# A selective-scan layer whose group loop is tied chunk by chunk: context products in mid tile, the second x tile turned into scan buffers, six stores in place of twenty

## The chip, the core and the metric

The kernel runs on one core of a Trainium2 chip. The core has five engines that run side by side, each through its own queue in order: TensorE (PE in the profile; PEld is its weight load), VectorE (DVE), ScalarE (ACT), GpSimd (POOL) and SyncE (SP), which here issues DMA transfers. The metric is the device time of one execution, in microseconds (us).

## The reference

One attention layer and one bidirectional state-space (SSD) layer over 1024 latent positions, with 256 context positions ahead of them, model width 1024. The change lies in the SSD layer, which is, cut to what matters:

```python
z, xbc, dt_raw = jnp.split(h @ w_in, ...)              # front, for context and latent
xbc = silu(centred_depthwise_conv(xbc, conv_w, conv_b))   # 5 taps
xs, bm, cm = jnp.split(xbc, ...)                       # 8 groups: x 256, B 128, C 128 columns each
dt = softplus(dt_raw + dt_bias)
# per direction d, in chunks of 128 positions:
a_cs   = jnp.cumsum(dt * A, axis=chunk);  a_last = a_cs[:, :, -1]
states = einsum(bm, exp(a_last - a_cs), xs * dt)
h      = exp(a_last) * h + states                      # from the context's final state
y      = einsum(cm @ bm.T * exp(a_cs_q - a_cs_s), xs * dt) + einsum(cm, h_prev, exp(a_cs))
u = rms_norm_per_group((y_fwd + y_bwd + d_skip * xs) * silu(z))
h = h + gate * ((u * norm_w) @ w_out)
```

## The kernel before

Everything is fp32; each product is made of three passes over a high and a low part (`uH`, `uL` of the input, `wh`, `wl` of the weights). Layer 0 and the making of `uH` and `uL` fill the span up to some 747 us and are not touched. Then comes the SSD layer in 8 groups of 4 heads.

A group has a *front* (function `front`) and a *scan* (`slot`, once for each of 8 chunks). The front makes four tiles, in the order `bT` (B), kind 0 and kind 1 (the two halves of x) and `cT` (C): for each but `cT` 24 products of 128x256 for the context into the one PSUM buffer `psD` (line 1085), and 48 products of 128x512 for the latent part into one of the two large buffers `pj2` (L1095, shown as pj). ScalarE and VectorE then apply the taps (L1007, L1011) and the SiLU (`silu`: a tanh on ScalarE back into the PSUM tile, L1018, and a product on VectorE, L1019), after which the PSUM tile's content is no longer wanted. The scan needs B and x with positions on partitions. So the tile is transposed on TensorE (L1058) and copied out by ScalarE (L1061): `natural` writes the transposes back into the tile's own `pj2` buffer, half a tile, copy, other half, copy. After the four tiles z follows, two times 96 products of 128x256 (L1129), each into a `pj2` buffer. So the first z tile needs the buffer of kind 1, and the second that of `cT`.

The scan of a chunk (`slot`) has on TensorE the scores product `pcb` (L1247), two products with the carried states `po` (L1249, L1250), the state product `S` (L1256), four products `yd` (L1281), and two transposes of the chunk before (L1312), all in the three small PSUM buffers `psX`; around them VectorE multiplies the decay tile `M` by the scores (L1251), merges two loaded rows into `M` (`merge`, L1230), GpSimd scales x (`xweight`, L1173) and states (`decay`, L1178), ScalarE takes exponentials of `M` (L1236). Context and backward states of a group (`states`: L1198 into `psD`, then the decay on GpSimd and an addition on VectorE, L1210) are made ahead, one at each `tick`.

The order: the front of group g+1 runs beside the scan of group g. `front` yields the cost of each product, and `run` takes products until a chunk's share is spent; a queue (`post`) pays out the work of the other engines as that cost grows, and work marked with a number (`LATE`, 3.0 us) comes out that much queue time later. This gives each instruction a place and priority; a scheduler then orders each engine's queue by priority and by when it reckons operands to be there, so rows move against the written order. `issue_after(x)` forbids the scheduler to put an instruction ahead of x. It is a rule on the order of issue; it adds no wait of its own.

The beginning of the layer is different: group 0's front runs alone, and beside it the step sizes dt are worked out (`dt_chain`). Their running sums go to DRAM in 8 stores (`decay`, L941), then come 12 small stores of the chunks' total decays (`total`, L951 and L952) and one load that spreads these over all partitions into `eal` (L953). Then `rows` loads M and bw of the first two chunks (L1221). The bw tiles get an offset on GpSimd (L1226) before they are merged.

Of the kernel before, what the change touches and what calls it, by code (L numbers as in the profile page):

```python
# [17 lines left out]
P = 128  # L18
# [15 lines left out]
R = 4  # L34
# [26 lines left out]
POST = 0.5  # L61
LATE = 3.0
DTPACE = 1.0
SEGS = (1.5, 2.0, 2.0, 2.2, 2.2)
# [47 lines left out]
class Kernel:  # L112
# [812 lines left out]
    def dt_chain(self, keep, rows):  # L925
# [11 lines left out]
        def decay():  # L937
            for o in (0, 384):
                for y in range(4):
                    d, s = y // 2, (o // 384) * 512 + 256 * (y % 2)  # L940
                    nc.sync.dma_start(self.acs_d[32 * d : 32 * d + 32, s : s + 256], w3[32 * y : 32 * y + 32, o : o + 256])  # L941
# [16 lines left out]
        def turn(b):  # L958
# [35 lines left out]
            lambda: act(ea, w3, AF.Exp),  # L994
            rows,
        ]
# [18 lines left out]
    def silu(self, raw, acc):  # L1015

        nc = self.nc
        return [lambda: nc.scalar.activation(raw, acc, AF.Tanh),  # L1018
                lambda: nc.vector.scalar_tensor_tensor(acc, in0=raw, scalar=1.0, in1=acc, op0=ALU.add, op1=ALU.mult)]  # L1019

    def front(self, g, st, post, first=None, dt=None):
# [30 lines left out]

        def natural(raw, acc, dst, o, n):
            steps = []

            def tr(lo, hi):
                for x in range(lo, hi):
                    nc.tensor.transpose(raw[:, x * P : (x + 1) * P], acc[:, x * P : (x + 1) * P], self.ident)  # L1058

            def ev(d, lo, hi):  # L1060
                nc.scalar.copy(d[:, :, o : o + P], raw[:, lo * P : hi * P].rearrange("p (c n) -> p c n", n=P))  # L1061

            for d, lo, hi in dst:
                steps.append(lambda lo=lo, hi=hi: tr(lo, hi))
                steps.append(lambda d=d, lo=lo, hi=hi: ev(d, lo, hi))
            return [(LATE, steps)]

# [8 lines left out]
        for n, (x, kind) in enumerate(tiles):  # L1076
# [3 lines left out]
            wh, wl = cur["h"], cur["l"]  # L1080
            if nat:
                raw = t(ps, [P, 512], F32, "psD")[:, :CTX]
                for k in range(KT):
                    for y, (l, r) in enumerate(((wh, uH), (wh, uL), (wl, uH))):
                        nc.tensor.matmul(raw, l[:, k, :], r[2][:, k, :], start=k + y == 0, stop=k == KT - 1 and y == 2)  # L1085
                        yield N256
                acc = t(pf, [P, CTX], F32, "cctx")
                post.extend(self.taps(x, raw, acc, 0, CTX, CTX) + self.silu(raw, acc) + natural(raw, acc, [(st[nat[0]][2], 0, 2)], nat[1], 2))
            raw = t(ps, [P, LAT], F32, "pj2")
            acc = t(pf, [P, LAT], F32, "cacc") if nat and kind != "bT" else t(p, [P, LAT], F32, kind)  # L1090
            for q in ((0,), (1,)) if g == 0 and n == 0 else ((0, 1),):
                for k in range(KT):
                    for y, (l, r) in enumerate(((wh, uH), (wh, uL), (wl, uH))):
                        for i in q:
                            nc.tensor.matmul(raw[:, 512 * i : 512 * i + 512], l[:, k, :], r[i][:, k, :], start=k + y == 0, stop=k == KT - 1 and y == 2)  # L1095
# [12 lines left out]
            post.extend(self.taps(x, raw, acc, 0, LAT, LAT) + self.silu(raw, acc))  # L1108
            if nat:
                post.extend(natural(raw, acc, [(st[nat[0]][i], 4 * i, 4 * i + 4) for i in range(2)], nat[1], 8))  # L1110

            def done(kind=kind, acc=acc):
                st[kind] = acc

            post.append((LATE, [done]) if nat else done)
        need(w)
        w0, w = w, loads[-1]()
        post.extend(w["steps"])
        for i in range(2):
            pj = t(ps, [P, 4, 256], F32, "pj2")  # L1120
            for q in range(2):
                ww = (w0, w)[q]
                need(ww)
                for c in range(4):
                    for k in range(4):
                        u, v = uH[i][:, 4 * q + k, c * P : (c + 1) * P], uL[i][:, 4 * q + k, c * P : (c + 1) * P]
                        for y, (l, r) in enumerate(((u, ww["h"]), (u, ww["l"]), (v, ww["h"]))):

                            nc.tensor.matmul(pj[:, c], l, r[:, k, :], start=c % 2 + q + k + y == 0, stop=c % 2 == 1 and q == 1 and k == 3 and y == 2)  # L1129
                            yield N256  # L1130
# [14 lines left out]
    def ssd(self, c0):  # L1145
# [31 lines left out]
        def decay(hn, h, g, c, d):  # L1177
            nc.gpsimd.tensor_tensor(hn, h, self.eal[:, hd(d, g), c].unsqueeze(2).broadcast_to([P, R, HP]), op=ALU.mult)  # L1178

# [58 lines left out]
        def slot(n, st, fill, tick):  # L1238
# [102 lines left out]
        offset(0, bw[0])  # L1341
        merge(fw[0], bw.pop(0))
        for half in range(2):
            decays(0, fw[0], half)
        self.tail = None
        with ExitStack():
            for g in range(G):
# [10 lines left out]
                def run(until):  # L1358
                    nonlocal spent
                    while spent < until:  # L1360
                        cost = next(work, None)
                        if cost is None:
                            return
                        spent += cost
                        post.run(cost)

# [22 lines left out]
    def ssd_out(self, p, spare, sp, sc, post):  # L1389
# [107 lines left out]
        for n, (i, mg, qs) in enumerate(sweeps):  # L1497
# [8 lines left out]
            for q in qs:  # L1506
# [5 lines left out]
                for z in range(2):  # L1512
# [11 lines left out]
                    for x in range(4):  # L1524
                        sl = slice(x * P, (x + 1) * P)
                        for y, (l, r) in enumerate(((w["h"], hi), (w["h"], lo), (w["l"], hi))):
                            nc.tensor.matmul(banks[x], l[:, z, sl], r, start=k == 2 * qs[0] and y == 0, stop=k == 2 * qs[-1] + 1 and y == 2)  # L1527
                            yield N512
# [165 lines left out]
```

## Time and profile before

| | us |
|---|---|
| median of three runs (1806.79, 1809.46, 1813.08) | 1809.46 |
| profiled execution | 1807.02 |
| its span | 1805.3 |
| around the span | 1.7 |

The span is what the profiler saw, from the first instruction to the last. Of the span, TensorE is busy 96%, VectorE 65%, ScalarE 48%, GpSimd 44%. A row such as "PE pj L1129 <- ACT xn L1061: 9.1, 7, 1.3" says that products of line 1129 waited for ScalarE's copy of line 1061, 9.1 us in all, 7 times, the longest 1.3 us. In a row of the chain stand the start, the length and the work: "1030.35 2.66 PE pj L1129 x20" are 20 products from 1030.35 us on. A row of stretches has, after its bounds, its length, then the busy time of PE, PEld, DVE, ACT and POOL, then the granted clock of TensorE (1.00 is full), the DMA share and rate.

### The profile page before, as it was taken

The page shows a single profiled execution, that of the slowest core. Times are in us where ns is not written, and L with a number is a line of the kernel's source. Part 1 is how long each engine was busy: PE and PEld are TensorE (multiplying, and loading weights), DVE is VectorE, ACT ScalarE, POOL GpSimd, SP SyncE. Part 2 cuts the span into 40 slices and gives each one's busy share as a digit, 9 for nine tenths or more (in the row PEclk, how much of TensorE's full clock was granted, in tenths as well). Part 3 has the DMA queues.
Part 4 walks back from the last instruction along what each step waited for, and adds up shares of the span by engine and source line. Part 5 has one row for each costly group of instructions (what it writes and reads, how often), then busy time and mean ns, then how long its engine had stood idle before and what let it go on. Part 6 is the DMA issues. An engine that isn't in the chain of part 4 may idle for free.

```text
span 1805.3 us, 28983 instructions
## 1 busy us (share of the span) xinstructions
PE 1739.6 (96%) x10319; PEld 1494.7 (83%) x10319; DVE 1181.8 (65%) x2115; ACT 867.1 (48%) x1906; POOL 799.0 (44%) x1068
## 2 busy tenths in 40 slices
PE   6899999999999999999999999999999999999997
PEld 2697788888888887778888898988889898888887
DVE  4634436778877885684776858577684867766734
ACT  3612237777777774452443525344353534544522
POOL 2331127555575545103454544645454464554411
PEclk9999999999999999999999999999999999999999
DMA  9558856444455436222222323222332322656533
GB/s 334 226 144 268 283 177 149 106 100 111 111 153 130 120 102 221 73 53 73 71 77 82 92 62 98 79 71 79 81 93 62 100 73 76 174 169 170 175 101 121
DMA packets 212495, 227.61 MB, mean 126 GB/s; under 512 B 16384, under 2 KB 149632, under 8 KB 212352
## 3 DMA queue, kind: packets, MB, share of 16 engines
q1 hardware_dynamic: 178288, 207.12, 38.0%
q0 software_dynamic: 34064, 18.65, 5.8%
q8 instruction: 81, 1.33, 0.3%
q14 instruction: 62, 0.51, 0.1%
HBM read 190.88 MB, written 35.13 MB: 125 GB/s over the span
## 4 chain that ended last, share of the span: by engine, by line
PE 81%; DVE 9%; ACT 4%; DMA 3%; issue 2%; SPq 1%; POOL 1%; DVEq 0%; ACTq 0%; POOLq 0%
PE pj L1095 17%; PE pj L1129 10%; PE pj L1527 7%; PE pj L246 6%; PE pj L247 6%; PE pj L248 6%; PE psD L1085 4%; PE psX L1281 3%; PE pt L684 3%; PE psD L1198 2%; PE pv L691 2%; PE pv L690 1%; PE S L659 1%; PE S L658 1%; PE psX L1249 1%
## 5 line engine op out<-in xcount | busy, mean ns | idle before, releaser
L246 PE MATMUL pj<-uH,wh 128*128 128x512 f32 (+1 forms) x712 | 257.4, 363 | 9.0 <-ACT uH L470 6.3
L247 PE MATMUL pj<-uL,wh 128*128 128x512 f32 (+1 forms) x712 | 243.3, 342 | 0.5 <-POOL uL L707 0.4
L248 PE MATMUL pj<-uH,wl 128*128 128x512 f32 (+1 forms) x712 | 242.4, 341 | 1.4 <-POOL wl L231 1.4
L1095 PE MATMUL pj<-uH,wl 128*128 128x512 f32 x512 | 172.7, 405 | 0.0
L1095 PE MATMUL pj<-uH,wh 128*128 128x512 f32 x512 | 171.4, 405 | 1.2 <-ACT bn L1061 0.7
L1095 PE MATMUL pj<-uL,wh 128*128 128x512 f32 x512 | 169.2, 402 | 0.0
L246 PEld LDWEIGHTS pj<-uH,wh 128*128 128x128 f32 x712 | 135.6, 191 | 36.2 <-ACT uH L470 7.7
L1129 PE MATMUL pj<-wh,uH 128*128 128x256 f32 x512 | 150.3, 294 | 9.1 <-ACT xn L1061 9.1
L1173 POOL TENSOR_TENSOR xw<-xn,dtdec 128x256 f32<-128x256 f32 x144 | 92.9, 650 | 141.6 <-PE psD L1198 107.1
L1129 PE MATMUL pj<-wh,uL 128*128 128x256 f32 x512 | 152.7, 298 | 0.0
L248 PEld LDWEIGHTS pj<-uH,wl 128*128 128x128 f32 x712 | 135.0, 190 | 18.6 <-POOL wl L231 2.3
L247 PEld LDWEIGHTS pj<-uL,wh 128*128 128x128 f32 x712 | 135.8, 191 | 16.0 <-issue 3.0
L1129 PE MATMUL pj<-wl,uH 128*128 128x256 f32 x512 | 146.7, 287 | 0.0
L689 DVE TENSOR_TENSOR pl<-pt,ph 128x512 fp32r<-128x512 f32 x168 | 114.1, 688 | 47.2 <-ACT ph L688 46.2
L231 POOL TENSOR_TENSOR wl<-wr,wh 128x512 fp32r<-128x512 f32 x76 | 100.2, 1322 | 86.1 <-ACT wh L229 85.2
L663 DVE CUSTOM_DVE_ANT_0 sm<-S,mask,nsink 128x640 f32<-128x640 f32 (+2 forms) x160 | 119.2, 773 | 19.8 <-PE S L659 12.6
L665 ACT ACTIVATE sm<-sm,nm 128x640 f32<-128x640 f32 (+2 forms) x160 | 118.6, 742 | 16.6 <-DVE nm L663 15.9
L688 ACT CAST ph<-pt 128x512 fp32r<-128x512 f32 x168 | 97.5, 586 | 56.0 <-PE pt L684 52.7
L229 ACT CAST wh<-wr 128x512 fp32r<-128x512 f32 (+1 forms) x116 | 74.7, 648 | 87.7 <-PE pj L247 63.5
L1095 PEld LDWEIGHTS pj<-uH,wl 128*128 128x128 f32 x512 | 95.3, 188 | 19.2
L1095 PEld LDWEIGHTS pj<-uL,wh 128*128 128x128 f32 x512 | 95.4, 188 | 18.7
L1129 PEld LDWEIGHTS pj<-wh,uH 128*128 128x128 f32 x512 | 98.7, 193 | 13.5 <-ACT xn L1061 12.1
(339 smaller groups left out, 4810.8 us busy)
## 6 DMA issues: line engine op xcount, KB each, us to landing
wr<-w_x SPq DMA_DIRECT2D x32, 512.0 KB, 4.6
M<-acs SPq DMA_DIRECT2D x64, 256.0 KB, 4.9
bw<-acs SPq DMA_DIRECT2D x64, 256.0 KB, 5.5
wr<-w_sk SPq DMA_DIRECT2D x24, 512.0 KB, 3.8
wr<-wg SPq DMA_DIRECT2D x40, 256.0 KB, 4.5
qs<-q POOLq DMA_DIRECT2D x40, 256.0 KB, 3.9
wada<-w_ada SPq DMA_DIRECT2D x16, 512.0 KB, 7.2
wr<-wq SPq DMA_DIRECT2D x32, 256.0 KB, 3.0
```

Source lines behind the costliest of these rows:

```text
L231: (eng or nc.vector).tensor_tensor(l, raw, h, op=ALU.subtract)
L246: self.nc.tensor.matmul(ps, lh, rh, start=first and i == 0, stop=False)
L247: self.nc.tensor.matmul(ps, lh, rl, start=False, stop=False)
L248: self.last_mm = self.nc.tensor.matmul(ps, ll, rh, start=False, stop=last and i == n - 1)
L663: nc.vector.tensor_tensor_reduce(out=sm[:, :W], in0=Sv, in1=self.mask[:, m0 : m0 + W], scale=-SCALE, scalar=self.nsink[:, 4 * j + r : 4 * ...
L665: nc.scalar.activation(sm[:, :W], sm[:, :W], AF.Exp, bias=nm[:, r : r + 1], scale=-1.0, accum_out=sums[:, r : r + 1])
L688: nc.scalar.copy(ph, ptf)
L689: nc.vector.tensor_sub(pl, ptf, ph)
L1095: nc.tensor.matmul(raw[:, 512 * i : 512 * i + 512], l[:, k, :], r[i][:, k, :], start=k + y == 0, stop=k == KT - 1 and y == 2)
L1129: nc.tensor.matmul(pj[:, c], l, r[:, k, :], start=c % 2 + q + k + y == 0, stop=c % 2 == 1 and q == 1 and k == 3 and y == 2)
L1173: nc.gpsimd.tensor_tensor(xw, X(st, c).rearrange("p (r h) -> p r h", r=R), self.dtdec[:, c, hd(d, g)].unsqueeze(2).broadcast_to([P, R, HP] ...
L1527: nc.tensor.matmul(banks[x], l[:, z, sl], r, start=k == 2 * qs[0] and y == 0, stop=k == 2 * qs[-1] + 1 and y == 2)
```

## The change

It has six parts.

1. `decay`: the running sums go out in 4 stores of 64 rows in place of 8 of 32; `total`: the totals in 2 stores in place of 12. `eal` then has its columns in another order, which `EPOS` gives.
2. `rows` (the first M and bw loads) stands right behind the stores of the sums, ahead of the totals and of the steps after them.
3. The first `merge` is tied behind the last SiLU product.
4. `natural`: all transposes of a tile, then its two copies. For kind 1 alone (`apart`) each half is transposed into a `psX` buffer of its own, so that its `pj2` buffer is free as soon as the SiLU product is done; that step, and the mark that the tile is there (`done`), come 6.8 us of queue time later (`LAST`) rather than 3.0.
5. The context products of a tile come in the middle of its latent products (after the fourth of eight steps) rather than ahead of them, but for the first tile.
6. The chunk's `pcb` is tied behind the last product of the front, and all front work of a chunk behind the chunk's `pcb`.

```diff
+LAST = 6.8
+EPOS = (0, 1, 5, 6, 3, 4, 8, 9, 2, 7)
...
         def decay():
-            for o in (0, 384):
-                for y in range(4):
-                    d, s = y // 2, (o // 384) * 512 + 256 * (y % 2)
-                    nc.sync.dma_start(self.acs_d[32 * d : 32 * d + 32, s : s + 256], w3[32 * y : 32 * y + 32, o : o + 256])
+            for d in range(2):
+                for o in range(2):
+                    dst = self.acs_d[32 * d : 32 * d + 32, 512 * o : 512 * o + 512].rearrange("r (h n) -> h r n", h=2)
+                    nc.sync.dma_start(dst, w3[64 * d : 64 * d + 64, 384 * o : 384 * o + 256])
...
             act(et, tot, AF.Exp)
-            for y in range(4):
-                d, h = y // 2, y % 2
-                row = self.eal_d[0][32 * d : 32 * d + 32]
-                for o, c in ((0, 2 * h), (3, 4 + 2 * h)):
-                    nc.sync.dma_start(row[:, c : c + 2], et[32 * y : 32 * y + 32, o : o + 2])
-                nc.sync.dma_start(row[:, 8 + h : 9 + h], et[32 * y : 32 * y + 32, 2:3])
+            for d in range(2):
+                nc.sync.dma_start(self.eal_d[0, 32 * d : 32 * d + 32].rearrange("r (h k) -> h r k", h=2), et[64 * d : 64 * d + 64])
...
             decay,
+            rows,
             total,
...
-            rows,
...
-        def natural(raw, acc, dst, o, n):
+        def natural(raw, acc, dst, o, n, apart=False):
...
+            def turn(d, lo, hi):
+                out, q = (t(ps, [P, 512], F32, "psX"), lo) if apart else (raw, 0)
                 for x in range(lo, hi):
-                    nc.tensor.transpose(raw[:, x * P : (x + 1) * P], acc[:, x * P : (x + 1) * P], self.ident)
...
+                    nc.tensor.transpose(out[:, (x - q) * P : (x - q + 1) * P], acc[:, x * P : (x + 1) * P], self.ident)
+                return lambda: nc.scalar.copy(d[:, :, o : o + P], out[:, (lo - q) * P : (hi - q) * P].rearrange("p (c n) -> p c n", n=P))
...
+            if apart:
+                for d, lo, hi in dst:
+                    out = []
+                    steps.append(lambda d=d, lo=lo, hi=hi, out=out: out.append(turn(d, lo, hi)))
+                    steps.append(lambda out=out: out[0]())
+            else:
+                out = []
+                steps.append(lambda: out.extend(turn(d, lo, hi) for d, lo, hi in dst))
+                steps += [lambda x=x: out[x]() for x in range(len(dst))]
+            return [(LAST if apart else LATE, steps)]
...
+            if nat and g + n == 0:
+                yield from ctx()
...
                 for k in range(KT):
+                    if k == KT // 2 and nat and g + n > 0:
+                        yield from ctx()
...
-            post.append((LATE, [done]) if nat else done)
+            post.append((LAST if kind == 1 else LATE, [done]) if nat else done)
...
-            nc.tensor.matmul(pcb, st["bT"][:, cs], st["cT"][:, cs], start=True, stop=True)
+            with self.tc.issue_after(self.pe.ins):
+                self.opened = nc.tensor.matmul(pcb, st["bT"][:, cs], st["cT"][:, cs], start=True, stop=True)
...
-        merge(fw[0], bw.pop(0))
+        with self.tc.issue_after(self.silu_last.ins):
+            merge(fw[0], bw.pop(0))
...
-                        cost = next(work, None)
...
+                        with self.tc.issue_after(self.opened.ins):
+                            cost = next(work, None)
```

`self.pe` is the latest product of a front (or of the closing product), `self.silu_last` the latest SiLU product. No arithmetic is added or taken away.

What this does to the queues. Below, a name's number tells buffers apart; line numbers after the change are some 1 to 12 higher. First, TensorE at the hand-over from `cT` to z while group 1's scan runs. Before (L1095 is `cT`, pj_2526 kind 1's buffer, psD_11038 its context, L1256 S, L1281 yd, L1247 pcb):

```order
L1256 MATMUL psX_11313<-xw_11263,bn_2266_9618 128x256
...
L1058 MATMUL pj_2526_11107<-ident_63,cacc_11108 128x128 x4
...
L1281 MATMUL psX_11342<-xn_2263_9615,M_11131 128x64 x2
L1058 MATMUL psD_11038<-ident_63,cctx_11106 128x128 x2
...
L1247 MATMUL psX_11464<-cT_10161,bT_9663 128x128
L1058 MATMUL pj_2526_11107<-ident_63,cacc_11108 128x128 x4
L1249 MATMUL psX_11466<-hf_11314,cT_10161 128x256
...
L1129 MATMUL pj_2582_11401<-wh_11295,uH_2034_8170 128x256
```

And after:

```order
L1209 MATMUL psD_11344<-xw_11310,bn_2461_10684 128x256
...
L1209 MATMUL psD_11373<-xw_11342,bn_2461_10684 128x256
L1060 MATMUL psX_11298<-ident_63,cacc_11029 128x128 x4
L1060 MATMUL psX_11304<-ident_63,cacc_11029 128x128 x4
L1293 MATMUL psX_11321<-xn_2265_9603,M_11101 128x64 x4
L1140 MATMUL pj_2582_11380<-wh_11273,uH_2034_8170 128x256
```

Before, the transposes of kind 1 stood in two pieces a dozen rows apart, both in the buffer that z (L1129) takes over; now both stand at the end of `cT`, in two psX buffers, directly ahead of `yd` and z.

Second, SyncE's queue behind the scans of the step sizes. Before:

```order
L941 DMA acs_8737<-sz_8871 32x256 x8
L951 DMA eald_8741<-tot_8874 32x2 x2
L952 DMA eald_8741<-tot_8874 32x1
...
L1221 DMA M_9099<-acs_8737 128x4x128
L1221 DMA bw_9101<-acs_8737 128x4x128
L953 DMA eal_8736<-eald_8741 128x640
```

After:

```order
L943 DMA acs_8737<-sz_8871 2x32x256 x4
L1232 DMA M_9005<-acs_8737 128x4x128
L1232 DMA bw_9007<-acs_8737 128x4x128
L1232 DMA M_9009<-acs_8737 128x4x128
L1232 DMA bw_9011<-acs_8737 128x4x128
L950 DMA eald_8741<-tot_8874 2x32x5 x2
L951 DMA eal_8736<-eald_8741 128x640
```

The first loads of M and bw moved from behind 20 stores to behind 4.

Third, TensorE in the first chunk of group 0's scan. Before, the last states (L1198) are spread over the z products and the next group's first tile:

```order
L1198 MATMUL psD_9443<-xw_9420,bn_2161_8760 128x256
...
L1247 MATMUL psX_9601<-cT_9227,bT_8798 128x128
...
L1198 MATMUL psD_9464<-xw_9441,bn_2161_8760 128x256
...
L1198 MATMUL psD_9489<-xw_9462,bn_2161_8760 128x256
L1256 MATMUL psX_9607<-xw_9487,bn_2161_8760 128x256
L1281 MATMUL psX_9644<-xn_2158_8757,M_9099 128x64 x4
```

After:

```order
L1209 MATMUL psD_9442<-xw_9419,bn_2162_8761 128x256
L1106 MATMUL pj_2271_9610<-uL_2133_8671,wh_9527 128x512
L1106 MATMUL pj_2271_9610<-uH_2034_8170,wl_9529 128x512
L1209 MATMUL psD_9467<-xw_9440,bn_2161_8760 128x256
L1209 MATMUL psD_9488<-xw_9465,bn_2161_8760 128x256
L1209 MATMUL psD_9509<-xw_9486,bn_2161_8760 128x256
L1268 MATMUL psX_9595<-xw_9507,bn_2161_8760 128x256
L1293 MATMUL psX_9628<-xn_2158_8757,M_9005 128x64 x4
L1262 MATMUL psX_9591<-hb_2253_9511,cT_9213 128x256
L1091 MATMUL psD_9665<-uH_1654_6747,wh_9527 128x256
```

Before, some 20 products stood between each two of the last three states; now the last three, all through the one psD buffer, stand row on row, and the next context products (L1091) want the same buffer right behind.

More of the change, by code (lines that the diff above doesn't have):

```diff
@@ L1109, in front @@
             if nat:
-                post.extend(natural(raw, acc, [(st[nat[0]][i], 4 * i, 4 * i + 4) for i in range(2)], nat[1], 8))
+                post.extend(natural(raw, acc, [(st[nat[0]][i], 4 * i, 4 * i + 4) for i in range(2)], nat[1], 8, kind == 1))
             def done(kind=kind, acc=acc):
                 st[kind] = acc
-            post.append((LATE, [done]) if nat else done)
+            post.append((LAST if kind == 1 else LATE, [done]) if nat else done)
         need(w)
@@ L1360, in run @@
                     while spent < until:
-                        cost = next(work, None)
[L1362 to L1365, printed above, removed]
+                        with self.tc.issue_after(self.opened.ins):
+                            cost = next(work, None)
+                            if cost is None:
+                                return
+                            spent += cost
+                            post.run(cost)
                 def tick():
@@ L1526, in ssd_out @@
                         for y, (l, r) in enumerate(((w["h"], hi), (w["h"], lo), (w["l"], hi))):
-                            nc.tensor.matmul(banks[x], l[:, z, sl], r, start=k == 2 * qs[0] and y == 0, stop=k == 2 * qs[-1] + 1 and y == 2)
+                            self.pe = nc.tensor.matmul(banks[x], l[:, z, sl], r, start=k == 2 * qs[0] and y == 0, stop=k == 2 * qs[-1] + 1 and y == 2)
                             yield N512
```

26 lines of the change are left out of this document (10 added, 16 removed).

## The prediction

> **What bounds the kernel now.** I read the page first, then the stretches of the SSD layer, then TensorE's waits in it, then the chain and the timelines at the two places where TensorE stands.
>
> ```profile
> span 1805.3 us, 28983 instructions
> PE 1739.6 (96%) x10319; PEld 1494.7 (83%) x10319; DVE 1181.8 (65%) x2115; ACT 867.1 (48%) x1906; POOL 799.0 (44%) x1068
> PE 81%; DVE 9%; ACT 4%; DMA 3%; issue 2%; SPq 1%; POOL 1%; DVEq 0%; ACTq 0%; POOLq 0%
> L1095 PE MATMUL pj<-uH,wh 128*128 128x512 f32 x512 | 171.4, 405 | 1.2 <-ACT bn L1061 0.7
> L1129 PE MATMUL pj<-wh,uH 128*128 128x256 f32 x512 | 150.3, 294 | 9.1 <-ACT xn L1061 9.1
> ```
>
> TensorE carries the chain, and no product is added or removed. So only time in which TensorE stands, or runs at a lower clock, can be won or lost. Where that is, the stretches of the SSD layer tell (the change acts from about 747 to 1735 us):
>
> ```profile
> 780.00:800.00 20.00, 17.12 (x91) 13.87 (x90) 19.07 (x25) 10.58 (x14) 0.00 (x0) 1.00 0.15 39
> 800.00:820.00 20.00, 16.25 (x83) 12.53 (x81) 12.30 (x19) 11.73 (x41) 2.78 (x4) 0.95 0.47 84
> 820.00:840.00 20.00, 20.00 (x140) 19.24 (x141) 8.64 (x10) 3.21 (x5) 6.86 (x12) 0.88 0.16 53
> ...
> 955.60:1061.40 105.80, 104.50 (x651) 93.63 (x651) 72.77 (x124) 45.10 (x106) 53.04 (x74) 1.00 0.29 80
> ...
> 1590.30:1735.00 144.70, 144.67 (x688) 119.96 (x688) 88.28 (x133) 64.16 (x128) 55.07 (x64) 1.00 0.52 159
> ```
>
> A group of the steady loop is 105.8 us, of which TensorE is busy 104.50: it stands 1.3 us. The last group and the closing product (1590 to 1735) have no gap to win. The beginning (780 to 820) has 2.9 and 3.75 us of standing, and a granted clock of 0.95 and 0.88 just behind it. TensorE's waits in that layer say the same:
>
> ```profile
> PE pj L1129 <- ACT xn L1061: 9.1, 7, 1.3
> PE pj L1058 <- DVE cacc L1019: 2.9, 2, 2.3
> ```
>
> Seven groups times 1.3 us is the one steady wait, z's first product behind a copy of the second x tile.
>
> **Part A: that tile turned into buffers of its own, and later.** The chain through one of the seven shows what z waits for:
>
> ```profile
> 1024.02 0.44 PE pj L1058 x4
> ...
> 1026.16 0.88 ACT M L1236 x3
> 1027.04 0.34 ACT uT L1313
> 1027.38 0.94 ACT wh L1034
> 1028.32 1.11 ACT cT L1007
> ...
> 1029.83 0.48 ACT xn L1061
> ...
> 1030.35 2.66 PE pj L1129 x20
> ```
>
> The second half's copy stands on ScalarE behind a weight cast, `cT`'s first tap and the rest, and z needs the buffer that it empties. After the change z needs only the SiLU product of that tile. When is that there? In the trace the tile's last product is issued at 1006.88 us, and then:
>
> ```profile
> 1006.88 0.24 PE pj L1095
> ...
> 1012.79 4.78 PE pj L1095 x21
> 1008.70 3.91 DVE L1011 SCALAR_TENSOR_TENSOR cacc<-pj,cw,cacc 128x1022 f32<-128x1022 f32 x3
> 1015.33 1.27 DVE L1011 SCALAR_TENSOR_TENSOR cacc<-pj,cw,cacc 128x1022 f32<-128x1022 f32 x1
> 1017.77 1.22 DVE L1019 SCALAR_TENSOR_TENSOR cacc<-pj,cacc 128x1024 f32<-128x1024 f32 x1
> ```
>
> The SiLU ends at 1018.99, 11.9 us behind the product's end at 1007.12. Its order on VectorE is little different after the change; I take 12.1. What TensorE has to do in that time: by the new order 48 products of `cT` at 4.78/21 = 0.228 us, 10.9, and of one chunk's scan `po`, `S` and two states (five products at 0.43, below), and the scores and three transposes, some 0.6 by four transposes' 0.44; together 13.7. So the transposes come about 1.6 us after their operand is there, and z behind them waits for nothing. The whole 9.1 us goes. The bounds: 0, if VectorE is over 2.9 us later than I count, and 10.3, because the pipeline also has to fill again behind each wait (the issue of products resumes 1.47 us late, not 1.3, as I read it from the starts on either side). I take 9.1, as the slack exceeds the difference of the two orders on VectorE. The two copies now hang behind the transposes, and what is late next is the next user of psX, a transposed y or the next `pcb`: by the order's rows they stand 4.8 and 5.6 us behind, cover enough for two copies of 0.48 us.
>
> **Part B: six stores, and the loads ahead of them.** In the beginning the chain leaves TensorE altogether:
>
> ```profile
> 795.98 0.42 SPq L941
> ...
> 803.40 3.08 DMA eald<-tot
> ...
> 807.07 9.10 DMA M<-acs
> ...
> 821.95 5.08 PE pj L1129 x30
> 827.46 3.83 PE pj L1129 x32
> POOL bw L1226 <- DMA bw<-acs: 72.6, 1, 72.6
> 815.05 0.73 DVE L1230 COPY_PREDICATED M<-before,bw 128x512 f32<-128x512 int32 x1 [5.26 <-POOL bw L1226]
> 815.92 1.22 DVE L1019 SCALAR_TENSOR_TENSOR cacc<-pj,cacc 128x1024 f32<-128x1024 f32 x1
> 814.26 0.62 PE L1095 MATMUL pj<-uH,wl 128*128 128x512 f32 x2
> 817.19 0.66 PE L1058 MATMUL pj<-ident,cacc 128*128 128x128 f32 x4 [2.31 <-DVE cacc L1019]
> ```
>
> The stores take SyncE from 795.9 to 803.4 us at 0.46 each (0.42 and the step to the next), the loads then need 9.1 us, GpSimd's offset and VectorE's merge wait for them, and behind the merge, in order, stands the SiLU of the second x tile. VectorE idles 5.26 us with that SiLU ready to run. TensorE has its last `cT` products out at about 814.7; then until 821.95 it does 8 transposes (0.44 for four), two of the context and two states (0.43 each), about 2.0 us of work in 7.2. So it loses 5.2 us there. After the change the merge stands behind the last SiLU, so this SiLU follows its taps, and the loads start 16 stores, some 7 us, earlier besides. z then waits for nothing. The gain: 5.2 us. The clock behind it: 30 products in 5.08 us at 0.169 each, against 32 in 3.83 at 0.120 right after: 30 x 0.049 = 1.5 us. If the stall goes, so does the dip; I take 1.1 of the 1.5, since the first products behind a transpose are slower anyway. Together 6.3; bounds 3 (another wait of some 2 us in the same place, and the dip with it) and 7.
>
> The four larger stores of sums carry twice the rows each. They are on the path from the scans to the merge alone, which now has slack of several us; no cost.
>
> [...]
>
> **Part C: `bT`, kind 0 and the context in mid tile, in the beginning.** All eight transposes now come ahead of two copies: TensorE is held up once and not twice (0.7 us by the row of L1095 above), but kind 1's first products wait for context transposes and copies that they did not wait for (about as much). I put this at 0, between -0.8 and +0.8. In the steady loop the mid-tile products only change places with others of the same tile.
>
> **Part D: group 0's states come later.** `done` at 6.8 moves the states back, so that the last ones stand row on row in the first chunk, through the one psD buffer. Each step there needs a product, VectorE's addition and GpSimd's decay, which wait for one another:
>
> ```profile
> L1178 POOL TENSOR_TENSOR hb<-hb,eal 128x256 f32<-128x256 f32 x49 | 34.4, 703 | 0.3 <-DVE hb L1210 0.3
> L1210 DVE TENSOR_TENSOR hb<-hb,psD 128x256 f32<-128x256 f32 x55 | 23.0, 418 | 74.2 <-PE psD L1198 70.9 <-POOL xs L1272 3.3
> 827.03 0.43 PE psD L1198 x2
> ```
>
> 0.70 + 0.42 and the hand-overs make 1.3 us a step. Four steps are 5.2; TensorE has in between two products, three states, `S`, `yd` and one `po`, about 3.0. So a new stall of 2.2 us, once. Bounds: 0 (the steps run ahead of the products) and 5.3 (all four steps bare, and the clock dips by 1.1).
>
> **Part E: the ties in the chunks.** They add no wait, only an order. I add up TensorE's rows by the durations above between each `pcb` and the next: before the distance goes from 6.8 to 19.0 us, after it is 12 to 14 us everywhere in the loop. From `pcb` to `yd`, which needs the multiplied decay tile, the shortest is 3.0 before and 3.5 after. But from `pcb` to `S` the shortest is 2.5 before and 1.1 after. Neither is waited for now:
>
> ```profile
> L1281 PE MATMUL psX<-xn,M 128*128 128x64 f32 x448 | 58.2, 268 | 0.0
> L1256 PE MATMUL psX<-xw,bn 128*128 128x256 f32 x98 | 29.1, 378 | 0.0
> ```
>
> `S` needs x scaled by GpSimd at the end of the chunk before, which with 44% busy is not late. I take 0; bounds 0 and 1 us a group, 7 us in all.
>
> **The sum.** -9.1 - 6.3 + 0 + 2.2 + 0 = -13.2 us on the profiled execution's 1807.0 (1805.3 and 1.7 around it): 1793.8. That execution is near the fastest of the three runs; on the median of 1809.5 the same sum gives 1796.3. I forecast 1795.0, between the two.
>
> **The rivals.** First, that the change misses its steady wait: the SiLU comes late, or the two psX buffers of the transposes come free late (psX has three, and scores, `po`, `S`, `yd` and the tail all pass through it), and z waits about as long as before. For it: the slack of 1.6 us is small beside an 11.9 us chain through two in-order engines. Against: the evenly spaced chunks leave these engines less crowded there. Then A is 0 and the rest -4.1: about 1805. A half of it gives 1800. Chance 0.16.
>
> Second, the beginning keeps a wait: D at its upper end takes back B. Then -9.1 - 3 + 5.3: about 1802. Chance 0.11.
>
> Third, on the other side: `S` or `yd` waits in every chunk. The order is now rigid: a product that is held up holds all the front's products of its chunk, where before the scheduler had put many between. If `S` waits for one more GpSimd instruction of the kind of 0.65 us (L1173, the scaling) in each of 56 chunks, that is 36 us, and the time is 1830. It decides from 13.2/56 = 0.24 us a chunk, and is slower by more than 0.3% from 0.33.
>
> ```profile
> L1173 POOL TENSOR_TENSOR xw<-xn,dtdec 128x256 f32<-128x256 f32 x144 | 92.9, 650 | 141.6 <-PE psD L1198 107.1
> ```
>
> For it: 1.1 us from `pcb` to `S`. Against: GpSimd waits for TensorE in that row, not the other way round. A smaller wait of 0.35 a chunk gives about 1815. Chance 0.15.
>
> **How the numbers follow.** My forecast has 0.58: 1788 to 1801 by its bounds. What a measurement of this kernel can tell from no change is about 0.3%, 5.4 us, so faster is below 1804. Faster takes my case, the second rival's better part and half of the first: 0.73. Same takes the full first rival and the rest: 0.12. Slower: the third, 0.15. The range for 8 in 10 goes from 1787 to 1812: it leaves out the larger part of the third rival, and a little below.
>
> **What would show it.** In the profile after: z's first products without a wait for a copy, and a loop period of 104.3 to 104.5 (A); TensorE without the gap of 5 us ahead of the first z, clock 1.00 behind it (B); in the first chunk of group 0 a wait of states, or of the context product behind them, for VectorE's addition, about 2 us (D); no wait of `S` and `yd` (E). I am wrong if a wait of TensorE appears that recurs in each chunk or each group, above all for psX buffers or GpSimd.

## The result, and the profile after

| | median of runs, us | profiled execution: span | SSD layer: its first product at | from there to the span's end |
|---|---|---|---|---|
| before | 1810.65 (1806.79 to 1813.08, 4 runs) | 1805.3 | 747.86 | 1057.4 |
| after | 1790.12 (1787.68 to 1793.67, 4 runs) | 1786.8 | 746.71 | 1040.1 |

The ratio is 0.9889, with a 95% interval from 0.9872 to 0.9905: some 20 us faster, between 17 and 23. (Two of all the executions below lie far outside, 1921.51 us with group 0 marked ready early and 3467.46 us with bT in psX too, and the ratios leave them out.) The forecast was 1795.0, in a range from 1787 to 1812. The two profiled executions lie 18.5 us apart. Of these 1.15 stand ahead of the SSD layer, in work that the change does not touch; the layer itself is 17.3 us shorter. That last column turns out to be the sharp measure here, and the experiments below use it: the start is the row of the first context products in the chain ("747.86 3.13 PE psD L1085 x24" before, "746.71 3.13 PE psD L1091 x24" after).

From the page of the changed kernel, the groups, and from its stretches:

```profile
span 1786.8 us, 28991 instructions
PE 1733.4 (97%) x10319; PEld 1493.5 (84%) x10319; DVE 1197.2 (67%) x2115; ACT 874.4 (49%) x1906; POOL 799.0 (45%) x1068
L1140 PE MATMUL pj<-wh,uH 128*128 128x256 f32 x512 | 150.4, 294 | 0.0
...
780.00:800.00 20.00, 17.18 (x98) 14.53 (x97) 18.27 (x24) 10.77 (x16) 0.00 (x0) 1.00 0.16 46
800.00:820.00 20.00, 20.00 (x126) 17.83 (x125) 15.91 (x20) 10.81 (x38) 2.97 (x5) 1.00 0.47 115
820.00:840.00 20.00, 20.00 (x159) 19.63 (x158) 6.59 (x10) 5.34 (x9) 7.41 (x11) 1.00 0.16 41
840.00:860.00 20.00, 18.71 (x98) 15.44 (x97) 10.65 (x25) 4.09 (x11) 12.17 (x17) 1.00 0.17 46
1019.10:1123.10 104.00, 104.00 (x652) 93.75 (x652) 75.50 (x124) 46.03 (x106) 53.29 (x75) 1.00 0.30 82
```

z's wait of 9.1 us is gone (0.0), a steady group has TensorE busy for 104.00 of 104.00 us, where it was 104.50 of 105.80, and from 800 to 840 us it neither stands nor slows down. The largest of TensorE's waits that are left between the layer's first product and the closing ones:

```profile
PE psD L1209 <- DVE hb L1221: 1.2, 2, 0.6
PE pj L1106 <- ACT bn L1061: 1.2, 1, 1.2
PE psD L1091 <- ACT xn L1061: 1.1, 1, 1.1
```

z's first product, by its rows in TensorE's timeline, gives the difference by stretch (before at 821.77, 924.58 and 1559.25 us for groups 0, 1 and 7, after at 813.01, 915.02 and 1539.28). A steady period is 104.04 (1019.12 and 1123.12 are two of them, 104.00 apart; the next four lie 104.04 apart) against 105.78.

| stretch | before | after | difference |
|---|---|---|---|
| first product of the layer to group 0's first z | 73.9 | 66.3 | -7.6 |
| to group 1's | 102.8 | 102.0 | -0.8 |
| to group 7's, six periods | 634.7 | 624.3 | -10.4 |
| to the end of the span | 246.05 | 247.5 | +1.5 |

The last row is mostly order and not a loss: by TensorE's rows a chunk's scores, its two products `po` and two transposes more, and a state less, stand behind group 7's first z after the change, some 0.9 us.

At the hand-over to z the slack is what the prediction had worked out. From the timelines of VectorE and TensorE:

```profile
1014.40 1.23 DVE L1018 SCALAR_TENSOR_TENSOR cacc<-pj,cacc 128x1024 f32<-128x1024 f32 x1 [0.28 <-ACT pj L1020]
1017.43 1.04 PE L1060 MATMUL psX<-ident,cacc 128*128 128x128 f32 x8
1018.30 1.00 PE L1293 MATMUL psX<-xn,M 128*128 128x64 f32 x8
1019.12 0.36 PE L1140 MATMUL pj<-wh,uH 128*128 128x256 f32 x1
```

The SiLU ends at 1015.63 and the transposes start 1.8 us later (1.6 was forecast). And the new stall at the last states of group 0 is there as drawn, each step being an addition that waits for a product and a product that waits for the addition:

```profile
847.29 0.70 PE L1209 MATMUL psD<-xw,bn 128*128 128x256 f32 x2
848.58 0.70 PE L1209 MATMUL psD<-xw,bn 128*128 128x256 f32 x2 [0.58 <-DVE hb L1221]
849.86 0.70 PE L1209 MATMUL psD<-xw,bn 128*128 128x256 f32 x2 [0.58 <-DVE hb L1221]
```

The steps are 1.28 us, where a product takes 0.43: two of them lose 1.7 us. The first starts 0.51 us behind the product before it (846.78), where 0.23 is usual, so some 0.3 is lost there: 2.0 in all, against 2.2 forecast.

So the parts that the prediction named are found where it put them. Whether they are there for its reasons is another matter.

### The profile page after: what moved, and what is told of

Read it like the earlier page. It is cut to its first block, busy times and chain, and to the rows that moved or that the text cites. A ratio compares the mean times of both kernels' runs of the same rounds, so it can differ in the third digit from the quotient of the medians.

```text
span 1786.8 us, 28991 instructions
## 1 busy us (share of the span) xinstructions
PE 1733.4 (97%) x10319; PEld 1493.5 (84%) x10319; DVE 1197.2 (67%) x2115; ACT 874.4 (49%) x1906; POOL 799.0 (45%) x1068
## 4 chain that ended last, share of the span: by engine, by line
PE 84%; DVE 9%; issue 2%; ACT 2%; DMA 2%; POOL 0%; SPq 0%; DVEq 0%; ACTq 0%; POOLq 0%
PE pj L1106 18%; PE pj L1140 10%; PE pj L1541 7%; PE pj L248 7%; PE pj L249 6%; PE pj L250 6%; PE psD L1091 4%; PE psX L1293 3%; PE pt L686 3%; PE psD L1209 2%; PE pv L693 2%; PE psX L1262 2%; PE psX L1261 2%; PE pv L692 2%; PE S L661 1%
## 5 line engine op out<-in xcount | busy, mean ns | idle before, releaser
L250 PEld LDWEIGHTS pj<-uH,wl 128*128 128x128 f32 x712 | 135.0, 190 | 18.5 <-POOL wl L233 2.1
L1325 ACT ACTIVATE uT<-psX,nw 128x128 f32<-128x128 f32 x128 | 46.6, 364 | 171.6 <-PE psX L1324 170.7
```

The source lines that it names most:

```text
L250: self.last_mm = self.nc.tensor.matmul(ps, ll, rh, start=False, stop=last and i == n - 1)
```

## The experiments

Those named *without* are the changed kernel with one thing undone, those named *alone* the kernel before with one thing done. "Layer" is the time from the SSD layer's first product to the span's end in the profiled execution, as above; the ratio is that to the kernel before, with its interval.

| kernel | median, us | ratio | layer, us | against |
|---|---|---|---|---|
| without the tile in psX | 1810.65 | 1.0007 (0.9989 to 1.0024) | 1058.1 | +18.0 on after |
| without the tie of the front's work | 1816.5 | 1.0044 (1.0030 to 1.0059) | 1067.9 | +27.8 |
| without the context in mid tile | 1821.56 | 1.0067 (1.0045 to 1.0089) | 1068.2 | +28.1 |
| without the tie of the scores | 1792.07 | 0.9906 (0.9884 to 0.9928) | 1040.1 | 0.0 |
| without the tie of the first merge | 1792.02 | 0.9906 (0.9888 to 0.9925) | 1040.1 | 0.0 |
| with twenty stores again | 1790.57 | 0.9903 (0.9884 to 0.9923) | 1039.9 | -0.2 |
| group 0 marked ready early | 1793.62 | 0.9921 (0.9898 to 0.9943) | 1040.1 | 0.0 |
| bT in psX too | 1792.47 | 0.9904 (0.9887 to 0.9921) | 1040.0 | -0.1 |
| ties alone | 1855.5 | 1.0259 (1.0236 to 1.0283) | 1104.9 | +47.4 on before |
| turning alone | 1815.55 | 1.0040 (1.0024 to 1.0056) | 1066.9 | +9.5 |
| context in mid tile alone | 1810.48 | 1.0014 (1.0001 to 1.0027) | 1057.8 | +0.3 |
| beginning alone | 1804.85 | 0.9978 (0.9964 to 0.9992) | 1053.5 | -3.9 |

### First set: one thing undone at a time

Theory: the second x tile's own buffer was what z waited for, so psX carries the gain of the loop; ties and context products only order. Rivals: the even chunks carry it, or the context's place.

**The tile in its own buffer again** (`u_turn`).

```diff
-natural(..., nat[1], 8, kind == 1)
+natural(..., nat[1], 8)
-post.append((LAST if kind == 1 else LATE, [done]) if nat else done)
+post.append((LATE, [done]) if nat else done)
```

> The changed kernel, but the second x tile (kind 1) is turned as the other tiles are: eight transposes back into its own pj2 buffer, then two copies, all 3.0 us of queue time behind the SiLU. Theory (the buffer held by the copies is what z waits for): z's first product waits for a copy again in each of 7 groups, the loop's period goes from 104.04 us back to 105.3 to 105.6, and the time is 9 to 10 us above the changed kernel's. Rival (the even chunks made ScalarE free at that place): z waits for less than 0.3 us, the period stays under 104.4, and the time is within 2 us of the changed kernel's.

TensorE's first rows of waits:

```profile
PE pj L1140 <- ACT xn L1061: 10.9, 5, 2.9
PE pj L1541 <- ACT wh L1473: 1.8, 1, 1.8
```

The wait is back, so the theory's mechanism holds. But its size is not the old one: 2.9 us in groups 2, 4 and 6, with periods of 107.1 and 104.2 in turn, and 1.7 and 0.6 in groups 0 and 1. All of the gain is gone with it, 18.0 us of 17.3, not 9 to 10. A part is the 1.8 us for a weight cast in the closing product, and at one of the five waits the clock falls (0.66 on average from 1450 to 1460 us), so that the last period is 106.95 without a wait at its end.

ScalarE's timeline shows why every second group is spared. For z at 1030.34 the transposes are through at about 1026.9, but the copies start at 1029.24: ahead of them stand a weight cast (1025.62, 1.06 us), exponentials (1.27) and `cT`'s first tap (1.19). For z at 1134.55 the cast stands behind the copies (1134.79), and these start at 1133.44, 0.3 us behind the transposes. The run undoes the buffers and the later time (3.0 for 6.8) together; which of the two the gain needs is not separated.

**The front's work not tied** (`u_run`).

```diff
-                        with self.tc.issue_after(self.opened.ins):
-                            cost = next(work, None)
+                        cost = next(work, None)
```

> The changed kernel without the tie of the front's work to the chunk's scores (the tie of the scores to the front's last product stays). Theory (the ties only order, the turn into psX carries the gain): no wait at z, period 104.0 to 104.4, time within 2 us of the changed kernel's; the three states of group 0 that stand row on row are spread again, so the 2.2 us stall there goes. Rival (even chunks keep the waits of small products hidden): waits of S, yd or the scores come back, 0.5 us a group or more, period over 104.5, time 3 to 8 us higher.

```profile
PE pj L1106 <- DVE wl L1039: 2.4, 4, 0.6
PE psD L1209 <- ACT hx L1213: 2.4, 1, 2.4
PE psX L1268 <- POOL xw L1184: 2.2, 3, 0.7
...
1500.00:1600.00 100.00, 93.88 (x585) 83.52 (x584) 75.39 (x130) 51.10 (x117) 51.56 (x69) 0.97 0.52 153
1600.00:1740.00 140.00, 136.52 (x639) 113.11 (x638) 80.29 (x122) 57.56 (x117) 59.09 (x65) 0.98 0.50 146
```

The theory falls here, and the rival's 3 to 8 us is far too little. z hardly waits (0.3 us in three groups), yet the layer is 27.8 us longer: the ties do not merely order. The order of rows tells why. The scheduler now lets the front run ahead of the scan: by TensorE's starts, 31 to 33 us lie between the first and the second scores of groups 1 to 6 (43.4 at the last group), and 7 to 17 between the others; in the changed kernel all lie 11 to 14 us apart behind group 0. In the crowded chunks `S` waits for GpSimd, states for ScalarE, products for their weights. The period is 101.4 and 111.5 in turn, and most of the loss falls at the end: from group 7's first z to the last product of the kernel it is 257.8 us against 239.3, with 6.1 and 3.5 us of standing in the two stretches shown, where the changed kernel has 0.0 and 0.45. In the last group the closing product fills the scan; 150 of its products run between the first two scores, where the changed kernel has 39, and it waits for weights (1.9 us) and later for its inputs (1.4). The waits that were not there before and the clock, at 0.50 for 13.7 us, make up some 22 of the 27.8; the rest is spread and not assigned.

**The context ahead of its tile** (`u_ctx`).

```diff
-            if nat and g + n == 0:
+            if nat:
                 yield from ctx()
-                    if k == KT // 2 and nat and g + n > 0:
+                    if False:
```

> The changed kernel with a tile's context products ahead of its latent ones again. Theory (they only change places): period 104.04 within 0.2, time within 2 us of the changed kernel's. Rival (the 0.27 us a group that the loop gained beyond z's wait of 1.47 comes from the context products in mid tile): period 104.25 to 104.4, time 1.5 to 2.5 us higher; or more, where a wait for psD or pj2 shows.

```profile
PE psD L1091 <- ACT xn L1061: 17.6, 8, 3.2
```

This falls as well; of the rival only its last clause holds, a wait for psD. A context product at the head of a tile finds the one psD buffer still holding the context of the tile before, until ScalarE has copied it. It stands for it once a group, 2.0 us in four groups, 2.7 in two and 3.2 in one (the eighth wait in the row, 1.1, is in the beginning, and the changed kernel has it too). These are 16.5 of the 28.1 us, and at four of them the clock falls to 0.50, for 17 us in all. In mid tile this wait is covered by half a tile of latent products.

**Group 0 marked ready early** (`v_last0`).

```diff
-            post.append((LAST if kind == 1 else LATE, [done]) if nat else done)
+            post.append((LAST if kind == 1 and g else LATE, [done]) if nat else done)
```

and the same for the turning step.

> The changed kernel with group 0's second x tile marked ready at 3.0 us of queue time rather than 6.8. By part D of the prediction (the later mark pushes group 0's states together): the stall of 2.2 us at the first chunk's last three states goes, time 2 us lower. Rival (the ties of the first chunk push them together): the stall stays at 2.2 us and the time within 0.5 us.

```profile
PE psD L1209 <- DVE hb L1221: 1.2, 2, 0.6
```

The stall is unchanged. Part D had the right stall and nearly its size, but the mark at 6.8 is not its cause.

### Second set: one thing alone, and the beginning's halves

The theory by then: a tied order shows every wait that the scheduler had covered by moving rows, and the turning and the context's place take these waits out of the tied order; none of the three would do alone.

**The ties alone** (`d_ties`).

```diff
-            nc.tensor.matmul(pcb, ...)
+            with self.tc.issue_after(self.pe.ins):
+                self.opened = nc.tensor.matmul(pcb, ...)
...
+                        with self.tc.issue_after(self.opened.ins):
                             cost = next(work, None)
```

> The kernel before with the two ties of a chunk alone (scores behind the front's last product, front work behind the scores). Theory after the first four runs (a tied order shows every wait that the scheduler had covered by moving rows): z waits 2.9 us for the copy of kind 1's own buffer, and a context product at a tile's head waits 2.8 us for psD, both in each of 7 groups; period 108 to 112 us against 105.78, time 15 to 35 us above before. Rival (the ties cost nothing by themselves and even out the chunks): period 105 to 106, time within 3 us of before.

```profile
PE pj L1058 <- ACT bn L1061: 11.6, 7, 1.8
PE pj L1129 <- ACT xn L1061: 9.5, 5, 3.2
PE pj L1058 <- ACT xn L1061: 8.2, 7, 2.2
PE psD L1198 <- ACT hx L1202: 5.5, 2, 2.7
...
PE psD L1085 <- ACT xn L1061: 2.8, 1, 2.8
```

47.4 us slower, beyond the 15 to 35 expected; the periods behind the first lie between 111.3 and 113.2. There is one more wait than was thought of: the second half of a tile's transposes waits for the copy of the first half (L1058 for L1061, 1.7 and 1.2 us a group on average), since both go through the same buffer step by step. In the run with the tile in its own buffer again, which has all transposes ahead of both copies, no such row is left. The wait at a context's head came only once. And the clock is a large part: TensorE stands 38.4 of the 800 us from 820 on, and over the same 800 us its granted clock is 0.97 on average.

**The turning alone** (`d_turn`): `natural`, `apart` and `LAST` as in the change, all else as before.

> The kernel before with the new turning of tiles alone: all transposes ahead of the copies, kind 1 into psX, 6.8 us later. Theory (z's wait hung on the buffer alone): no wait at z, period 104.1 to 104.6, time 8 to 11 us below before. Rival (without the ties the scheduler's moves bring small waits elsewhere, as in the run without the tie of the front's work): z's wait gone, but waits of S, states or weights of 0.5 us and more take its place, period 105.5 to 107, time not below before.

```profile
PE psD L1204 <- POOL xw L1179: 5.0, 1, 5.0
PE pj L1533 <- DVE uL L1539: 3.1, 1, 3.1
PE pj L1533 <- DVE uH L1539: 1.8, 1, 1.8
```

z's wait is gone from all groups, and the mean of the seven periods falls from 105.4 to 103.0. Nonetheless the layer is 9.5 us longer: in the last group the time from the first z to the last product is 264.0 us against 238.3. It is the picture of the kernel without the front's tie: here too the front runs ahead, 18 us between the first two scores of group 1, growing to 33 at group 6 and 47.7 at the last group, where 166 closing products run in that place and later ones wait for their inputs (3.1 and 1.8 above). The theory that z's wait hung on the buffer is right; that taking it away is worth its length is not. The wait of 5.0 us is the beginning's, moved from z to the states.

**The first merge not tied** (`u_merge`) and **twenty stores again** (`u_stores`), each in the changed kernel.

```diff
-        with self.tc.issue_after(self.silu_last.ins):
-            merge(fw[0], bw.pop(0))
+        merge(fw[0], bw.pop(0))
```

> The changed kernel without the tie of the first merge, which then stands ahead of the second x tile's SiLU again; six stores and early loads kept. Theory (the loads, some 7 us earlier, are there before the SiLU could run): no wait ahead of the first z, time within 1 us of the changed kernel's. Rival (the tie does it): VectorE idles 1 to 5 us ahead of the merge, TensorE's gap ahead of the first z is back by 1 to 5 us.

`u_stores` has the 8 and 12 stores of the kernel before, with the loads still behind the first 8 and `eal`'s columns in the old order.

> The changed kernel with the twenty stores, the M and bw loads still right behind the sums' eight and the first merge still tied. Theory (the merge's place alone matters): no wait ahead of the first z, the first chunk's scan finds M merged, time within 1 us of the changed kernel's. Rival (the stores' time on the queue matters): the loads land 2 to 4 us later and the first chunk's products or the states' decays wait 2 to 5 us more.

Neither moves the layer by more than 0.2 us, and in both TensorE has no gap ahead of the first z. In the run without the tie the merge does stand ahead of the SiLU (807.30 and 810.37 on VectorE), but its rows are there in time: VectorE idles 1.2 us for them, not 5.26. So for the beginning the early loads are enough without the late merge. Whether the late merge is enough without them was not run: the twenty stores leave the loads behind the first eight. The fewer stores by themselves are worth nothing that can be seen.

### Third set: the rest

**The beginning alone** (`d_start`): six stores, the loads ahead of the totals, and the tie of the first merge, in the kernel before.

> The kernel before with the beginning's three parts alone (six stores, loads ahead of the totals, first merge tied). Theory (part B stands by itself): the gap ahead of the first z goes, with the clock's dip; the loop's period stays at 105.78 and z's wait of 1.3 us with it; time 5 to 7 us below before. Rival (the beginning's gain is given back, since the last states then crowd the first chunk): less than 2 us.

```profile
PE pj L1129 <- ACT xn L1061: 9.4, 8, 1.3
PE pj L1058 <- ACT xn L1061: 1.4, 1, 1.4
```

-3.9 us in the layer, a ratio of 0.9978: less than the 5 to 7 of the theory, more than the rival's 2. The long gap goes and the period stays at 105.76, as the theory says, but the place gives something back: ahead of group 0's z the second half's transposes now wait for the first half's copy (1.4), and that z itself for a copy (0.24, the eighth of the waits).

**The context in mid tile alone** (`d_ctx`), the edit of part 5 in the kernel before.

> The kernel before with the context products in mid tile alone. Theory (without ties the scheduler covers psD either way, so they only change places): period 105.5 to 106.1, z's wait still there, time within 3 us of before. Rival (any one part alone hurts, as the ties alone and the turning alone did): 5 us or more above before.

+0.3 us, period 105.70, z's wait there: with a free order it makes no difference in the layer, as part C said. (The runs' ratio of 1.0014 is not found there.)

**The scores not tied** (`u_pcb`): the changed kernel with the front's work still tied behind the scores, but the scores free to move ahead.

```diff
-            with self.tc.issue_after(self.pe.ins):
-                self.opened = nc.tensor.matmul(pcb, ...)
+            self.opened = nc.tensor.matmul(pcb, ...)
```

> The changed kernel without the tie of the chunk's scores to the front's last product; the front's work is still tied behind the scores. By the order only one chunk of a group then starts early (7 us behind the one before it, and the next 20). Theory (of the two ties the one of the front's work carries the gain): period 104.0 to 104.6, time within 4 us of the changed kernel's. Rival (the early chunk's small products wait): period over 105, time 7 us and more above it.

Period 104.06, layer 1040.1: this tie is worth nothing; the one of the front's work carries it.

**bT through psX as well** (`v_bt`), an attempt at a better version.

```diff
-natural(..., nat[1], 8, kind == 1)
+natural(..., nat[1], 8, kind == 1 or (g == 0 and kind == "bT"))
```

> The changed kernel with group 0's first tile (bT) turned into psX buffers too. By its order the first x tile no longer waits for the copies of bT (1.3 us), and of the three states that stood row on row only the last two do (of the 2.2 us some 1 us left). Theory: TensorE's waits in the beginning go from 6.8 to some 4 us, the time 2 to 3 us below the changed kernel's, hardly more than its runs scatter. Rival: the psX buffers are then missing for the step sizes' transposes in the beginning, and a wait of 1 to 3 us comes there; no gain.

```profile
PE psX L962 <- DVE xn L992: 2.1, 1, 2.1
...
PE psD L1209 <- DVE hb L1221: 0.6, 1, 0.6
```

The rival: the wait for `bn` is gone and the states' stall is down to one step, but the step sizes' transposes wait 2.1 us that were not there. The layer is 1040.0, no gain. No version here beats the changed kernel.

## Why the prediction was right, and where its steps failed

The direction and the range were right; the gain was put at 14 and is 20 us (17 to 23), of which the layer shows 17.3. That the sum came near is in part luck: Part A was too small, and Part E's 0 came out only because other parts of the change, not counted for it, cover what the tie exposes.

**Part A, z's wait.** The wait went, with the slack that was worked out. It was mis-sized: 1.3 us a group by idle time, while the period fell by 1.74. Of that 1.47 is what the issue of products lost at the wait, the upper bound that the prediction had and did not take. By TensorE's starts it is rather 1.55: z's first product starts 1.58 us behind the transpose ahead of it, where such a pair takes 0.03 elsewhere. Another 0.2 is lost once a group at a `yd`: in the kernel before it starts 0.36 us behind `S`'s second product rather than 0.22 (1094.26, released by VectorE's L1260, which ends at 1094.20), and the next product is 0.05 late; after the change no `yd` starts so late behind `S`. The prediction had "neither is waited for now" there, from rows that show 0.0. The two come to the 1.74; what else shifts is smaller and of both signs. "The whole 9.1 us goes" is therefore too little: the six steady periods alone give 10.4.

**Part A, its condition.** The step that failed in its reasoning is that the tile's own buffers were enough. Alone they made the kernel 9.5 us slower. The prediction added the parts up one by one, but they work as a set: turning, context in mid tile and the front's tie. With any one of the three undone, the layer is 18 to 28 us longer than with all, and no better than before.

**Part B, the beginning.** -7.6 us to the first z, of which 1.1 is two states (0.43 each) and two context transposes that moved behind it: 6.5 against 5.2 forecast, 0.6 of it part C's. The clock behind it, from 820 to 840 us, stays at 1.00, where it was 0.88. That a first product behind a transpose is slower shows in the trace after, at a clock of 1.00: the next one starts 0.20 us behind it (813.01 and 814.19 us), where 0.12 is usual. The stated cause, "behind the merge stands the SiLU", is right, but the merge's new place is not needed: the early loads, which the prediction named "besides", are enough. (SyncE's stores begin at 794.12, not at 795.9 as it read.) Where z still waits for its copy, only 3.9 us of the beginning's gain remain, as the beginning alone shows.

**Part C.** "Only change places" holds in a free order (+0.3) and fails in the tied one, where psD's one buffer costs 2.0 to 3.2 us a group. In the beginning, put at 0, the waits for copies and SiLUs of the first tiles fall by 0.6, from 3.4 to 2.8 us.

**Part D.** Right stall, 2.0 us for 2.2; wrong cause. Neither the mark at 6.8 (unchanged without it) nor the ties alone make it; it is gone without the front's tie, which is thus needed for it but not enough, and smaller where bT goes through psX. It hangs on where the scheduler puts the last states, and what decides that was not isolated.

**Part E.** "They add no wait, only an order. I take 0" is the step that failed most. In the sum it did no harm, since the finished order has no waits of `S` or `yd`. But the tie of the front's work is worth 27.8 us in the changed kernel and costs 47.4 together with the other tie in the old one (alone it was not run there). The count of TensorE's rows that the prediction made (12 to 14 us from scores to scores, instead of 7 to 19) was the sign of it, and was read as harmless rather than, as the rows suggest, as what keeps the last group's scan covered. The third rival, that a rigid order shows waits in every chunk, is what happens with the ties alone; its place was the transposes and z, not `S`.

## What to carry to other kernels

An order that is tied by hand and the removal of the waits that it exposes belong together: costed one at a time each looks like nothing or worse, and each undone alone can take the whole gain with it. Where a scheduler moves rows, look at how evenly the bound engine's work covers the helper chains right to the last stage, since what has run ahead is missing at the end. A part that shows no wait in the finished profile is not thereby free to drop: undo it before saying that it is worth nothing.

## What was unexpected of the hardware

*The clock behind a wait.* The kernel without the tile in psX has the same wait of 2.9 us in several groups. Its stretches around and behind three of them:

```profile
1020.00:1040.00 20.00, 17.11 (x116) 15.56 (x115) 15.46 (x22) 8.04 (x16) 11.19 (x17) 1.00 0.23 60
1240.00:1250.00 10.00, 8.28 (x61) 8.01 (x62) 8.53 (x13) 3.64 (x10) 4.60 (x8) 1.00 0.33 96
1450.00:1460.00 10.00, 7.12 (x35) 6.76 (x34) 7.34 (x7) 4.98 (x13) 3.34 (x5) 0.66 0.34 108
```

The first two leave the clock at 1.00, the third drops it to 0.66 on average over 10 us. In the kernel before, z's waits of 1.3 us are followed by 1.00 (955.60 to 1590 us), while the beginning, with 3.75 us of standing from 800 to 820 us and 2.31 us as its longest single wait, is followed by 0.50 from 820 to 825 us and by 1.00 from 825 on. So in these runs the length of a wait does not by itself tell whether the clock falls behind it. What else decides was not isolated.

*Where the runs scatter.* In all fourteen profiled kernels TensorE has the same rows in the same order ahead of the SSD layer, and yet they start that layer between 745.89 and 753.83 us, while the layer itself repeats: 1039.9 to 1040.1 us in the changed kernel and the five that equal it. The scatter of this kernel's runs is some 6 us; in these profiles, at least, it is that of the untouched first layer.
